# A decoder trunk on one core: recurrent weights split ahead of time in three feed-forward blocks, x copied on ScalarE in the first, and a bound on pending one-column products

## The chip, the cores and the metric

The kernel runs on one core of one Trainium2 chip. The metric is the device time of one execution in microseconds (us). Beside the timed runs there is a profile of one execution. Engine names are those of the profile: PE is TensorE's matmuls, PEld its weight loads, DVE is VectorE, ACT is ScalarE, POOL is GpSimd, SP issues nearly all DMAs.

## The reference, cut to what matters

The input x is 512 tokens by 1024. Two layers, each with a half-weighted SwiGLU, a mixer, and another half-weighted SwiGLU. The mixer of layer 0 is attention, that of layer 1 is RWKV-7 time mixing.

```
def swiglu(h, w_gate, w_up, w_down):
    return (jax.nn.silu(h @ w_gate) * (h @ w_up)) @ w_down      # 1024 -> 2816 -> 1024

for layer in range(2):
    x = x + 0.5 * swiglu(rms_norm(x, ffn_norm[layer, 0]), ...)  # blocks 0 and 2
    h = rms_norm(x, mix_norm[layer])
    x = x + (attention(h) if layer == 0 else rwkv7_time_mix(h, ...))
    x = x + 0.5 * swiglu(rms_norm(x, ffn_norm[layer, 1]), ...)  # blocks 1 and 3
```

In order of time the stages are: feed-forward block 0, attention, blocks 1 and 2, time mixing, block 3. `rwkv7_time_mix` multiplies by the matrices w_k, w_v, w_r, w_o, some small ones (w2, a2, g2), and the low-rank (LoRA) matrices w1, a1, g1. Everything is float32.

## The kernel before, in words

**Split operands.** A float32 matrix t is held as two parts, hi (a cast, on ACT) and lo = t - hi (on DVE). A product is three matmuls, hi by hi, hi by lo, lo by hi (`mm3`). Every weight must so be loaded, cast on ACT (L296) and subtracted on DVE (L297) before TensorE uses it. x stays on chip, transposed, as eight chunks of 128 rows by 512 tokens.

**A feed-forward block** (`ffn`, its order written out in `ffn_steps`). The first 256 columns of gate and up are done in four head steps `("s", kk)`, each with two chunks of x: eight products per chunk pair and bank, the sums of x that the later products need (`sums`, L581 to L587, and their split L331, L332), and the squares of the two chunks (L615) with eight one-column products against ones that add them up over the rows (these run as 16 records). After the fourth the scale of each token (`rstd`) is known, and the gated product u of the head follows (L632). The remaining 2560 columns are five tiles of 512. In each a tile of gate and up is formed by a seven-product scheme, a Winograd form of a 2 by 2 block product: products "1", "2", "6", "7", "5", "3", "4" in two halves each, with weights' sums formed on DVE (L293, the "add" operations) and results combined on DVE (L654). L668 is the copy of product "1" out of PSUM; the third bank pair that it empties is the one in which product "2" goes on. Between the halves stand the transposes of the tile before (`turn`, L691, split by L331 and L332) and its down products (`down`, L712 adds them to x). A full tile has 18 steps that take a weight: 14 halves and four down steps, in the order 1a 1b 2a 2b 6a d0 6b 7a d1 7b 5a 5b d2 3a 3b 4a 4b d3. A block has four head steps, 16 steps in the first tile, 18 in each of the next three, 16 in the last and six at its end.

**Work buffers.** `work()` hands out four SBUF buffers in turn, counted by `turn_of` from the start of the block. The head takes 14: four squares, eight for the sums, one for the gate, one for u. So product "1" of each tile (buffer p) gets number 14, the buffer that held the last t of the sums.

**Parking.** The time mixing needs its weights split, too. That is done ahead, inside feed-forward blocks, and the parts go to DRAM. `next_w` counts a turn at every weight step; `park_some` takes one operation out of `park_ops` at every `park_every`-th turn between 13 and 90. An operation is a pair of weight pieces (70 pieces, 35 pairs): SP issues the loads into one shared raw buffer (L202), ACT casts them (L242), DVE subtracts (L243), SP issues two writes of 512 KB (L246). Two more operations, "lora", do four chunks of the LoRA matrices each (L255 loads, L264 on ACT, L265 on DVE, L269 writes); they need `self.v`, the vectors that `rwkv_setup` makes after block 0. All use the same `park_room`: the sixth of ten buffers, and `pair`, which also takes two transposed activations of the last tile. Before, parking is on in blocks 1 and 2 at every fourth turn: two LoRA operations and 17 pairs in block 1, 18 pairs in block 2.

**x at the start of block 0.** x comes in rows of tokens. `turned(c)` transposes chunk c on TensorE (L353) into a PSUM bank and copies it to `self.x[c]` (L356, on DVE); `prep(c)` then makes the scaled parts from the same bank (L572 on ACT, L573 on DVE). Chunks 0 and 1 come ahead of the first products, each later one two chunks ahead.

**Order.** The instructions' order on each engine is set by a scheduler when the kernel is built, by its own model of the times; it respects the data and the `after` edges (order only, no wait between engines). Each engine then works through its queue in that order.

Of the kernel before, what the change touches and what calls it, by code (L numbers as in the profile page):

```python
# [22 lines left out]
NCH = D // P  # L23
# [26 lines left out]
class Trunk:  # L50
# [160 lines left out]
    def plan_parks(self, every):  # L211

        small = [i for i, tag in enumerate(self.wring) if tag == "r"]
        self.park_ops = [("lora", k) for k in range(0, NCH, 4)] if small else []
        self.park_ops += [small[j : j + 2] for j in range(0, len(small), 2)]
        self.park_every = every

    def park_some(self):
        self.park_turn += 1
        if self.park_ops and 12 < self.park_turn <= 90 and self.park_turn % self.park_every == 0:  # L220
            self.park(self.park_ops.pop(0))

    def park(self, which):

# [98 lines left out]
    def mm3(self, out, lhs, rhs, start, stop):  # L323

        mm = self.mm
        self.after(mm(out, lhs[0], rhs[0], start=start, stop=False), self.gate)
        mm(out, lhs[0], rhs[1], start=False, stop=False)
        self.last_mm = mm(out, lhs[1], rhs[0], start=False, stop=stop)

# [4 lines left out]
    def load_x(self):  # L334
        nc = self.nc
        xsrc = self.a["x"][0].rearrange("(b p) d -> p b d", p=P)
        ts = [self.t("xio", [4, 256], 4) for _ in range(4)]
        t = self.t("vecs", [2, P])

        nc.sync.dma_start(t[:32, 0], self.a["ffn_norm"].rearrange("l f (c p) -> (l f c) p", p=P))  # L340
        nc.scalar.dma_start(ts[0], xsrc[:, :, :256])
        self.prefetch(-1, 1)
        self.prefetch(0)
        for i in range(1, 4):
            self.after(nc.scalar.dma_start(ts[i], xsrc[:, :, i * 256 : (i + 1) * 256]), self.last_cast)
        self.prefetch(-1)
        self.name_vectors(t)
        self.spread_vectors(slice(0, 1))

        def turned(c):  # L350
            ps = self.bank("fd", 2)
            for b in range(4):
                nc.tensor.transpose(  # L353
                    ps[:, b * P : (b + 1) * P], ts[c // 2][:, b, (c % 2) * P : (c % 2 + 1) * P], self.ident
                )
            nc.vector.tensor_copy(self.x[c], ps)  # L356
            return ps

        self.turned = turned
# [182 lines left out]
    def ffn(self, gain, done=lambda c: None):  # L542
# [54 lines left out]
        def first(kk):  # L597
# [6 lines left out]
            for k in (2 * kk, 2 * kk + 1):  # L604
                for b in range(4):
                    block = (0, 3)[b // 2] if k < 4 else (1, 2)[b // 2]
                    rhs = tuple(t[:, (k % 2) * S :][:, :S] for t in w)
                    self.mm3(live["s"][b], x_part(k % 4, block, b % 2), rhs, k == 0, k == NCH - 1)
                if turned and k + 2 < NCH:
                    prep(k + 2)  # L610
                if k >= 4:
                    sums(k - 4)
# [3 lines left out]
            for e in range(2):  # L616
                for b in range(4):
                    col = 4 * (c + e) + b
                    self.mm(
                        live["sum"][:, col : col + 1], sq[:, e, b * P : (b + 1) * P], self.ones[:, 0:1],  # L620
                        start=True, stop=True,
                    )
# [7 lines left out]
            for b, ps in enumerate(live["s"]):  # L630
# [2 lines left out]
                    out=u[:, b], in0=ps[:, FIRST:], scalar=rstd[:, b : b + 1], in1=g[:, b], op0=ALU.mult, op1=ALU.mult  # L633
                )
            us[-1] = [u[:, b] for b in range(4)]

        def product(n, q, h):
            if not h:
# [1225 lines left out]
def trunk_kernel(ctx, tc, stop=5, start=0, **aps):  # L1864
# [2 lines left out]
              lambda: t.plan_ffn(1, 0), lambda: t.plan_rwkv(), lambda: t.plan_ffn(1, 1)]  # L1867
    for s in stages[start : stop + 1]:
        s()
    t.plan_parks(4)  # L1870
    t.load_x()
    gains = {(l, f): t.vec["ffn_norm"][:, (2 * l + f) * NCH :][:, :NCH] for l in range(2) for f in range(2)}
    mixg = [t.vec["mix_norm"][:, l * NCH : (l + 1) * NCH] for l in range(2)]
# [13 lines left out]
            t.turned(c)  # L1887
        t.turned = None
    for i in range(start, stop + 1):
        t.parking = i in (2, 3)  # L1890
        if i in (0, 2, 3, 5):
            t.ffn(gains[i // 3, int(i % 3 > 0)], *[t.store_x] * (i == stop))
        elif i == 1:
# [34 lines left out]
```

## Time and profile before

| | |
|---|---|
| timed runs, us | 2142.15, 2133.08, 2140.88 (median 2140.88) |
| the profiled execution, us | 2135.13 |
| its span, us | 2133.2 |
| mean granted TensorE clock | 0.987 |
| feed-forward matmuls | block 0 from 8.0 to 379.0; blocks 1 and 2 from 626.9 to 1366.2; block 3 from 1755.5 to 2126.0 |
| TensorE busy in 0 to 400 us, 600 to 1010, 1010 to 1380, 1750 to 2133 | 385.2, 389.1, 364.7, 374.3 us |

The table's times of the blocks come from the timeline of TensorE, the last row from windows. An engine that is "busy" is in an instruction; a weight load (PEld) overlaps the matmuls. A wait in brackets after an instruction of the timeline is the idle time of its engine just before it, with what ended it.

### The profile page before, as it was taken

The page shows a single profiled execution, that of the slowest core. Times are in us where ns is not written, and L with a number is a line of the kernel's source. Part 1 is how long each engine was busy: PE and PEld are TensorE (multiplying, and loading weights), DVE is VectorE, ACT ScalarE, POOL GpSimd, SP SyncE. Part 2 cuts the span into 40 slices and gives each one's busy share as a digit, 9 for nine tenths or more (in the row PEclk, how much of TensorE's full clock was granted, in tenths as well). Part 3 has the DMA queues.
Part 4 walks back from the last instruction along what each step waited for, and adds up shares of the span by engine and source line. Part 5 has one row for each costly group of instructions (what it writes and reads, how often), then busy time and mean ns, then how long its engine had stood idle before and what let it go on. Part 6 is the DMA issues. An engine that isn't in the chain of part 4 may idle for free.

```text
span 2133.2 us, 29169 instructions
## 1 busy us (share of the span) xinstructions
PE 2048.1 (96%) x11527; PEld 1639.8 (77%) x11527; DVE 1585.9 (74%) x1981; ACT 954.4 (45%) x1381; POOL 123.4 (6%) x165
## 2 busy tenths in 40 slices
PE   8999999999989999999999999999898999999998
PEld 6788888776877788877878888777566668888887
DVE  6778786467777888887798888556966557887784
ACT  5433443354335554444544444373634425433342
POOL 0000000211000000000000000112322100000000
PEclk9999999999989999999999999999989999999999
DMA  5333332421113468763255674536654332333321
GB/s 169 89 115 103 99 99 72 125 79 51 52 47 100 147 221 275 237 207 128 62 196 197 211 235 158 207 112 191 213 135 104 91 120 83 109 99 119 109 89 40
DMA packets 219296, 282.41 MB, mean 132 GB/s; under 512 B 45395, under 2 KB 135659, under 8 KB 219160
## 3 DMA queue, kind: packets, MB, share of 16 engines
q1 hardware_dynamic: 216520, 278.20, 41.4%
q10 hardware_dynamic: 2640, 2.36, 0.3%
q8 instruction: 91, 1.49, 0.3%
q14 instruction: 45, 0.37, 0.1%
HBM read 227.76 MB, written 54.59 MB: 132 GB/s over the span
## 4 chain that ended last, share of the span: by engine, by line
PE 77%; DVE 11%; DMA 5%; ACT 3%; issue 2%; SPq 1%; POOL 0%; DVEq 0%; ACTq 0%
PE fp L120 36%; PE fd L120 18%; PE am L120 7%; PE rm L120 4%; PE rq L120 2%; DVE parts L297 2%; PE wo L120 2%; DMA const<-in_ffn_w_up_dram 1%; PE rl L120 1%; PE rr L120 1%; DVE const L1601 1%; DVE wx L293 1%; DVE const L1607 1%; ACT parts L296 1%; PE fd L691 1%
## 5 line engine op out<-in xcount | busy, mean ns | idle before, releaser
L120 PE MATMUL fp<-parts,xs 128*128 128x512 f32 x2016 | 493.1, 393 | 13.2 <-DVE parts L297 9.0
L120 PEld LDWEIGHTS fp<-parts,xs 128*128 128x128 f32 x2016 | 377.6, 189 | 96.6 <-DVE parts L297 12.0
L120 PE MATMUL fd<-act,parts 128*128 128x512 f32 x1728 | 409.4, 390 | 2.5 <-DVE acts L332 1.6
L296 ACT CAST parts<-wx 128x1024 fp32r<-128x1024 f32 x224 | 233.6, 1051 | 349.9 <-PE fp L120 174.6
L120 PEld LDWEIGHTS fd<-act,parts 128*128 128x128 f32 x1728 | 323.7, 188 | 72.6 <-DVE acts L332 3.4
L297 DVE TENSOR_TENSOR parts<-wx,parts 128x1024 fp32r<-128x1024 f32 x224 | 271.8, 1220 | 73.2 <-ACT parts L296 73.1
L296 ACT CAST parts<-const 128x1024 fp32r<-128x1024 f32 (+1 forms) x192 | 198.2, 1033 | 262.0 <-PE fp L120 134.0
L120 PE MATMUL fp<-parts,xb 128*128 128x512 f32 x1152 | 291.3, 400 | 9.6 <-ACT wx L668 6.8
L297 DVE TENSOR_TENSOR parts<-const,parts 128x1024 fp32r<-128x1024 f32 (+1 forms) x192 | 229.5, 1197 | 59.4 <-ACT parts L296 54.3
L120 PEld LDWEIGHTS fp<-parts,xb 128*128 128x128 f32 x1152 | 216.8, 191 | 56.1 <-ACT wx L668 7.4
L654 DVE TENSOR_TENSOR wx<-fp,wx 128x1024 f32<-128x1024 f32 x140 | 168.7, 1218 | 30.0 <-PE fp L120 28.8
L712 DVE SCALAR_TENSOR_TENSOR const<-fd,const 128x512 f32<-128x512 f32 x160 | 108.4, 685 | 77.6 <-PE fd L120 77.4
L120 PE MATMUL fp<-parts,xa 128*128 128x512 f32 x576 | 145.0, 400 | 4.3 <-ACT xa L572 2.6
L120 PEld LDWEIGHTS fp<-parts,xa 128*128 128x128 f32 x576 | 110.2, 193 | 29.2 <-ACT xa L572 3.3
L120 PE MATMUL am<-xg,parts 128*128 128x512 f32 x384 | 99.4, 410 | 0.0
L416 POOL TENSOR_TENSOR ssum<-ssum,sq 128x512 f32<-128x512 f32 x14 | 23.0, 1646 | 1198.3 <-ACT sq L415 1197.9
L120 PEld LDWEIGHTS am<-xg,parts 128*128 128x128 f32 x384 | 72.0, 191 | 25.6 <-issue 9.9
L102 ACT ACTIVATE wx<-wx,const 128x512 f32<-128x512 f32 x80 | 53.5, 716 | 43.7 <-DVE wx L654 43.6
L242 ACT CAST acts<-wx 128x1024 fp32r<-128x1024 f32 (+2 forms) x37 | 37.1, 1004 | 68.4 <-DMA wx<-in_rw_wk_dram 18.3
L243 DVE TENSOR_TENSOR acts<-wx,acts 128x1024 fp32r<-128x1024 f32 (+2 forms) x37 | 42.9, 1162 | 24.5 <-ACT acts L242 24.5
L120 PE MATMUL rm<-xm,parts 128*128 128x512 f32 x252 | 60.8, 394 | 0.0
L331 ACT CAST act<-fd 128x512 fp32r<-128x512 f32 x80 | 43.7, 587 | 37.3 <-PE fd L691 37.1
(316 smaller groups left out, 2632.9 us busy)
## 6 DMA issues: line engine op xcount, KB each, us to landing
wx<-in_ffn_w_down_dram SPq DMA_DIRECT2D x72, 512.0 KB
parts<-acts SPq DMA_DIRECT2D x68, 512.0 KB
parts<-parts SPq DMA_DIRECT2D x68, 512.0 KB
wx<-in_ffn_w_gate_dram SPq DMA_DIRECT2D x44, 512.0 KB
wx<-in_ffn_w_up_dram SPq DMA_DIRECT2D x40, 512.0 KB
const<-in_ffn_w_up_dram SPq DMA_DIRECT2D x40, 512.0 KB
const<-in_ffn_w_gate_dram SPq DMA_DIRECT2D x36, 512.0 KB
const<-in_ffn_w_down_dram SPq DMA_DIRECT2D x16, 512.0 KB
```

The costliest lines, as they stand in the source:

```text
L102: ins = nc.scalar.activation(out, in_, func, **kw)
L120: return self.pe(self.nc.tensor.matmul(*args, **kw))
L242: nc.scalar.copy(hi, src)
L243: nc.vector.tensor_tensor(out=lo, in0=src, in1=hi.bitcast(F32), op=ALU.subtract)
L293: self.nc.vector.tensor_tensor(out=out, in0=in0, in1=in1, op=ALU.add)
L296: self.last_cast = self.nc.scalar.copy(hi[:r, :n], raw[:, :n])
L297: self.nc.vector.tensor_tensor(out=lo[:r, :n], in0=raw[:, :n], in1=hi[:r, :n].bitcast(F32), op=ALU.subtract)
L331: self.nc.scalar.copy(hi, t)
L416: nc.gpsimd.tensor_tensor(out=ssum, in0=ssum, in1=sq, op=ALU.add)
L654: add = lambda out, other, ps=ps: nc.vector.tensor_tensor(out=out, in0=ps, in1=other, op=ALU.add)
L691: nc.tensor.transpose(ps[:, b * P : (b + 1) * P], us[n][b][:, f * P : (f + 1) * P], self.ident)
L712: nc.vector.scalar_tensor_tensor(out=self.x[c], in0=ps, scalar=0.5, in1=self.x[c], op0=ALU.mult, op1=ALU.add)
```

## The change: parking in three blocks, copies on ScalarE, an order edge and a skipped buffer

- `plan_parks` keeps the LoRA operations in a list of their own, and the step is 6 turns instead of 4. Parking is on in blocks 0, 1 and 2. `park_some` takes a LoRA operation first, once `self.v` is there, that is from block 1 on. With turns 18, 24, ... 90 this makes 13 pairs in block 0, two LoRA operations and 11 pairs in block 1, and 11 pairs in block 2.
- `turned` copies x out of PSUM on ScalarE instead of VectorE.
- An order edge on TensorE: the first product of head step kk comes after the last one-column product of head step kk - 2, so that no more than sixteen one-column products are pending.
- After the head, one work buffer is skipped: the tiles' p, q, v and r each take the buffer after the one they had. p then has the buffer of the last squares.

```diff
     def plan_parks(self, every):
         small = [i for i, tag in enumerate(self.wring) if tag == "r"]
-        self.park_ops = [("lora", k) for k in range(0, NCH, 4)] if small else []
-        self.park_ops += [small[j : j + 2] for j in range(0, len(small), 2)]
+        self.park_ops = [small[j : j + 2] for j in range(0, len(small), 2)]
+
+        self.lora_ops = [("lora", k) for k in range(0, NCH, 4)] if small else []
         self.park_every = every

     def park_some(self):
         self.park_turn += 1
-        if self.park_ops and 12 < self.park_turn <= 90 and self.park_turn % self.park_every == 0:
-            self.park(self.park_ops.pop(0))
+        ops = self.lora_ops if self.lora_ops and hasattr(self, "v") else self.park_ops
+        if ops and 12 < self.park_turn <= 90 and self.park_turn % self.park_every == 0:
+            self.park(ops.pop(0))
...
-        self.after(mm(out, lhs[0], rhs[0], start=start, stop=False), self.gate)
+        self.first_mm = self.after(mm(out, lhs[0], rhs[0], start=start, stop=False), self.gate)
...
-            nc.vector.tensor_copy(self.x[c], ps)
+            nc.scalar.copy(self.x[c], ps)
...
                     self.mm3(live["s"][b], x_part(k % 4, block, b % 2), rhs, k == 0, k == NCH - 1)
+                    if k == 2 * kk and not b:
+                        self.after(self.first_mm, live.get(("sq", kk - 2)))
...
-                    self.mm(
+                    live["sq", kk] = self.mm(
                         live["sum"][:, col : col + 1], sq[:, e, b * P : (b + 1) * P], self.ones[:, 0:1],
...
             us[-1] = [u[:, b] for b in range(4)]
+
+            next(turn_of)
...
-    t.plan_parks(4)
+    t.plan_parks(6)
...
-        t.parking = i in (2, 3)
+        t.parking = i in (0, 2, 3)
```

## The prediction

> **What bounds the kernel now.** I read the page first (busy shares and the chain), then windows over equal work in the four feed-forward blocks, then the timeline of single engines where a block is longer than the others.
>
> ```profile
> span 2133.2 us, 29169 instructions
> PE 2048.1 (96%) x11527; PEld 1639.8 (77%) x11527; DVE 1585.9 (74%) x1981; ACT 954.4 (45%) x1381; POOL 123.4 (6%) x165
> PE 77%; DVE 11%; DMA 5%; ACT 3%; issue 2%; SPq 1%; POOL 0%; DVEq 0%; ACTq 0%
> ```
>
> TensorE is busy 96% of the span. A change that removes no matmul can win only the stretches in which TensorE idles or runs below its clock. The change touches only the feed-forward blocks (blocks 0 to 3 in order of time). A window from the same product to the last product of each shows how much there is. The columns are the stretch, its length, then busy time and count for PE, PEld, DVE, ACT and POOL, then the granted clock, the DMA share and GB/s.
>
> ```profile
> 72.55:378.95 306.40, 304.08 (x1379) 251.07 (x1377) 238.93 (x253) 125.42 (x144) 6.61 (x4) 1.00 0.33 99
> 686.30:1007.60 321.30, 309.87 (x1378) 252.04 (x1377) 267.50 (x322) 155.66 (x218) 0.00 (x0) 0.99 0.61 198
> 1054.60:1366.20 311.60, 306.77 (x1378) 250.99 (x1377) 254.33 (x262) 138.97 (x160) 6.85 (x5) 1.00 0.60 197
> 1816.90:2126.10 309.20, 306.48 (x1396) 253.01 (x1396) 230.52 (x239) 115.97 (x131) 0.00 (x0) 1.00 0.30 91
> ```
>
> PE does 1378 or 1379 products in the first three (the fourth has some of the output's transposes too), so the lengths compare. Blocks 0 and 3 park nothing; against block 0, block 1 is 14.9 us longer and block 2 is 5.2 us longer. Parking therefore costs 20.1 us in all today. The heads of the blocks (72 products each) differ as well:
>
> ```profile
> 45.90:72.50 26.60, 22.26 (x101) 17.59 (x101) 19.49 (x31) 16.10 (x22) 0.00 (x0) 0.94 0.14 40
> 661.20:686.30 25.10, 21.28 (x97) 17.68 (x96) 18.08 (x26) 15.95 (x21) 0.00 (x0) 0.86 0.21 64
> 1034.80:1054.60 19.80, 19.36 (x98) 16.01 (x97) 14.60 (x21) 11.33 (x16) 0.00 (x0) 1.00 0.16 46
> 1796.40:1816.90 20.50, 19.40 (x97) 16.01 (x96) 14.95 (x22) 12.41 (x17) 0.00 (x0) 1.00 0.20 57
> ```
>
> Against block 3's 20.5 us, block 0's head loses 6.1 us and block 1's 4.6 us. These two and the 20.1 us are all that the change can reach: 30.8 us, 1.4% of the span.
>
> **The copies of x in block 0 move from DVE to ACT.** Eight instructions. The price on DVE is the row of L356; the price on ACT is that of the only like copy, L751's 128x512 PSUM copy.
>
> ```profile
> L356 DVE COPY const<-fd 128x512 f32<-128x512 f32 x8 | 5.5, 687 | 6.7 <-PE fd L353 6.7
> L751 ACT COPY xout<-fd x7: 585/586/593, 2118.1 to 2127.6; 128x512 f32<-128x512 f32 x7
> 47.31 0.63 PE L353 MATMUL fd<-const,xio 128*128 128x128 f32 x4 [0.23 <-DVE xb L573]
> 50.02 0.68 DVE L356 COPY const<-fd 128x512 f32<-128x512 f32 x1
> 50.74 0.69 ACT L572 ACTIVATE xb<-fd,const 128x512 fp32r<-128x512 f32 x1 [0.21 <-DVE const L356]
> 51.48 1.20 PE L120 MATMUL fp<-parts,xb 128*128 128x512 f32 x4 [1.71 <-ACT xb L572]
> 53.23 2.11 PE L120 MATMUL fp<-parts,xb 128*128 128x512 f32 x8 [0.55 <-DVE xb L573]
> 57.81 1.01 ACT L668 COPY wx<-fp 128x1024 f32<-128x1024 f32 x1 [0.34 <-DVE xs L332]
> 58.87 7.33 PE L120 MATMUL fp<-parts,xb 128*128 128x512 f32 x24 [1.85 <-ACT wx L668]
> ```
>
> DVE loses 5.5 us and ACT gains 8 x 0.586 = 4.7 us. In the head ACT is busy 16.10 of 26.60 us, so it has the room. What matters is the chain: the transposes end at 47.94 and the copy starts only at 50.02, because DVE works through its queue; L572 starts exactly when the copy ends, and TensorE waits 1.71 us for it. On ACT the copy and L572 follow each other and that queue is out of the chain. I take from this the waits of 1.71, 0.55 and 0.23 = 2.5 us. The last wait of the head, 1.85 us, ends with L668, which waited for DVE's last split of the sums; with DVE lighter by the copies of this stretch I take 1.4 us of it, and 0.6 us of the slow 24 products behind it (7.33 us, against 5.75 in a row below). That is 4.5 us. The bounds are 6.1 us (the head becomes block 3's) and a loss of 1.2 us: two copies of 0.586 us now stand ahead of the first casts on ACT. I take none of that loss, since the operands there come late by DMA; the cover is this wait, and without it the first products start later:
>
> ```profile
> 14.49 1.05 ACT L296 CAST parts<-const 128x1024 fp32r<-128x1024 f32 x1 [4.20 <-DMA const<-in_ffn_w_up_dram]
> ```
>
> Queued behind a copy on ACT are the weights' casts; a copy waits for its transposes, and DVE's second half of each split waits for ACT.
>
> **One work buffer is skipped after the head.** The copy of the first product (L668) then goes to the buffer of the last squares, free after their 16 one-column matmuls, and no longer to that of the last sums, free after DVE's L332. In block 1:
>
> ```profile
> 666.65 1.84 PE L120 MATMUL fd<-const,wx 128*128 128x1 f32 x16
> 669.28 1.22 DVE L332 TENSOR_TENSOR xs<-wx,xs 128x1024 fp32r<-128x1024 f32 x1
> 669.95 1.28 ACT L98 ACT_TABLE_LOAD   x1
> 671.25 1.01 ACT L668 COPY wx<-fp 128x1024 f32<-128x1024 f32 x1
> 672.31 7.80 PE L120 MATMUL fp<-parts,xb 128*128 128x512 f32 x24 [3.82 <-ACT wx L668]
> 675.65 1.90 DVE L632 SCALAR_TENSOR_TENSOR wx<-fp,const,wx 128x256 f32<-128x256 f32 x4 [0.34 <-ACT wx L102]
> 1804.96 5.75 PE L120 MATMUL fp<-parts,xb 128*128 128x512 f32 x24 [1.10 <-ACT wx L668]
> ```
>
> The squares are read by 668.5, DVE ends at 670.50, and a table load then stands ahead of the copy. Freed earlier, the copy can start near 669, about 2.2 us sooner, and the 3.82 us shrink to 1.6. Late next is the gated product u (L632, ends at 677.55), for which TensorE's next transposes wait, so I take no more than 2.2 us. Bounds: 0 (the order on ACT stays) and 4.6 us. In block 3 L668 already waits for TensorE, and I take nothing there. The clock is the open part: 24 products took 7.80 us behind the 3.82 us wait and 5.75 us behind a wait of 1.10.
>
> The Trainium skill ("TensorE: Matmul & The Clock Gate", HAM oscillation) says that TensorE drops to its slow clock in gaps of more than about 3.4 us. By it a wait cut to 1.6 us would give back the 2.05 us of clock as well, and block 1's term would be 4.3 us, an estimate; but block 0's 1.85 us wait ought to have cost no clock, and the trace disagrees there (7.33 us). I stay with 2.2 us.
>
> **One-column products, at most sixteen pending.** The first product of the third and fourth pair now comes behind the sums two pairs earlier. In block 1 both sums came a moment late:
>
> ```profile
> 643.27 1.75 PE L120 MATMUL fp<-parts,xb 128*128 128x512 f32 x7
> 644.86 3.63 PE L120 MATMUL fd<-const,wx 128*128 128x1 f32 x32
> ```
>
> Sixteen of these 32 records move ahead of seven products, 1.6 us. The order is on TensorE itself, the work is the same, and the squares that they read were written earlier. Zero; the bounds are 1.6 us either way.
>
> **Parking.** 35 pairs and two LoRA steps of four chunks each. Before, every fourth turn: 2 LoRA and 17 pairs in block 1, 18 in block 2. After, every sixth turn from 18 to 90: 13 pairs in block 0, 2 LoRA and 11 pairs in block 1, 11 in block 2. The number of operations and DMAs stays. Their rows:
>
> ```profile
> L242 ACT CAST acts<-wx 128x1024 fp32r<-128x1024 f32 (+2 forms) x37 | 37.1, 1004 | 68.4 <-DMA wx<-in_rw_wk_dram 18.3 <-DMA wx<-in_rw_wv_dram 16.5 <-DMA wx<-in_rw_wr_dram 11.0
> L243 DVE TENSOR_TENSOR acts<-wx,acts 128x1024 fp32r<-128x1024 f32 (+2 forms) x37 | 42.9, 1162 | 24.5 <-ACT acts L242 24.5
> ACT acts L264 <- DMA lora<-acts: 12.2, 6, 5.2
> 737.81 4.38 PE L120 MATMUL fp<-parts,xs 128*128 128x512 f32 x11 [1.83 <-DVE parts L297]
> 745.05 2.81 PE L120 MATMUL fp<-parts,xs 128*128 128x512 f32 x11 [1.76 <-DVE parts L297]
> 225.00:250.00 25.00, 25.00 (x120) 20.80 (x119) 22.64 (x24) 11.46 (x14) 0.00 (x0) 1.00 0.20 57
> 1207.00:1232.00 25.00, 24.43 (x115) 19.84 (x113) 24.76 (x27) 13.55 (x16) 0.00 (x0) 1.00 0.52 168
> 768.00:865.00 97.00, 96.34 (x436) 79.23 (x435) 86.55 (x88) 46.79 (x51) 0.00 (x0) 1.00 0.69 233
> 768.00:865.00 97.00, 10.53 (x10) 1.00 0.69 233
> 1082.00:1107.00 25.00, 22.70 (x101) 17.82 (x100) 24.30 (x25) 11.23 (x13) 0.00 (x0) 1.00 0.39 124
> ```
>
> A pair costs ACT 1.0 us and DVE 1.16 us, and ACT stood 68.4 us before these casts with the weights' casts queued behind. The LoRA chunks share one room, so each waits for the write before it. I give the LoRA 6.5 us of block 1's 14.9: waits of 1.83 and 1.76, 1.57 of slow clock (4.38 less 2.81), some 1.3 around. It stays: eight serial chunks still cover the next tile's crowded part. The other 13.6 us (8.4 and 5.2) are 35 pairs at 0.39 us.
>
> The crowded part is the stretch from the first to the sixth of the block products: DVE is busy 24.76 of 25 us with parking, 22.64 without. So block 0 has 2.36 us of slack there, two splits' worth. At a flat 0.39 us the move costs 13 x 0.39 = 5.1 us in block 0 and returns 5.1 us in blocks 1 and 2; for that slack I take 1 us of gain. Bounds: 5.1 us of gain (block 0 hides them all), and 4.1 us of loss, if each of block 0's four tiles lost what block 2's worst tile did (25.00 less 22.70 = 2.3 us; 9.2 less 5.1). SP's queue carries 13 pairs' loads and writes more in block 0, where DMA is busy 0.33 against 0.61 and 0.60 in the windows above. The parking at turn 90 shares a buffer with the last tile's transposed activations; its write must land first. It has no row before, and I cost it 0, with up to 2 us in each of two blocks inside the bounds.
>
> **Sum.** 4.5 + 2.2 + 0 + 1.0 = 7.7 us. The profiled execution took 2135.1 us, the median of the runs is 2140.9, the other runs 2133.1 and 2142.2: the four have a mean of 2137.8, the profiled one 2.7 below. 2137.8 less 7.7 gives 2130 us (2127 for an execution like the profiled one, 2133 for one like the median).
>
> **Rivals.** *Parking spreads better than flat.* The waits come from bunches: at a third fewer in a block each finds its room free. If block 0 hides its 13 and blocks 1 and 2 drop by half of their 13.6 us: 6.8 + 6.7 = 13.5, 2124 us. Against it: the second row for 768 to 865 counts L242 alone: ten casts in 97 us, and TensorE lost only 0.66 us.
>
> *The heads don't move.* The scheduler orders ACT anew; a copy caught behind a cast that waits for its weights costs what DVE's queue cost. The heads give 0 to 1 us: 2137 us. For it: ACT's casts in the head also wait for DMA and TensorE; against it: 10.5 us of ACT idle there.
>
> *Slower: parking at one fixed place.* A tile has 18 steps and 6 divides 18, so in every full tile a parking falls on the second half of the second product, just ahead of the crowded part, where every fourth step wandered. Eleven such tiles (4, 3, 4) at block 2's 2.3 us are 25.3 us against 13.6 now: 11.7 more, less 6.7 of the heads, 2143 us. It decides from 1.85 us a tile. Against it: the tiles of the 97 us stretch.
>
> **How the numbers follow.** Forecast 0.45, better spread 0.22, heads unmoved 0.20, fixed place 0.13. A measurement tells about 0.5% here, 10.7 us: faster means under 2130.2. The forecast lies on that edge and gives 0.24 faster and 0.21 same; the spread is faster; the unmoved heads are same; the fixed place gives 0.07 same and 0.06 slower. Together 0.46, 0.48, 0.06. Range 2118 (both heads whole at 10.7, 5.1 of parking, and 4 of the runs' own scatter) to 2143 (the fixed place).
>
> **What would show it.** Copies: block 0's head window near 22 us and no wait on L572. Buffer: L668 in block 1 before 669.5. Parking: the window of block 0 from 306.4 to about 310, block 1's from 321.3 to about 318, block 2's to about 309; DVE waits at the first half of the sixth product in every tile would speak for the fixed place. I am wrong if the other stages move by more than 3 us, or if block 0 grows by more than 9.

## The result and the profile after

The changed kernel takes 2149.9 us (median of 8 runs, 2145.8 to 2156.6); the kernel before takes 2142.0 (8 runs, 2133.1 to 2145.5). The ratio is 1.0044, interval 1.0032 to 1.0055: slower by 8 us between the medians (9 us by the ratio), where 7.7 us of gain were forecast, and outside the range of 2118 to 2143. The two profiled executions differ by more, 2135.1 against 2150.1, because that of before lay 6.9 us under its own median and that of after at its median; in which stages those 6.9 us lie, no run tells. Medians and ratios leave out two executions of the experiments that took 6152.6 us (no90_q) and 11232 us (crowd).

The page of the changed kernel, the lines that answer to the first fence of the prediction:

```profile
span 2147.9 us, 29168 instructions
PE 2057.7 (96%) x11527; PEld 1645.2 (77%) x11527; DVE 1581.6 (74%) x1973; ACT 957.0 (45%) x1389; POOL 123.5 (6%) x165
PE 74%; DVE 14%; ACT 5%; DMA 4%; issue 2%; SPq 1%; POOL 0%; DVEq 0%; ACTq 0%; POOLq 0%
```

In the chain DVE has 14% for 11% and ACT 5% for 3%, although DVE's own work shrank (1585.9 to 1581.6 us). TensorE waits more often for the two engines that split weights. The windows of the changed kernel over the same products as in the prediction: the heads of blocks 0 and 1, then the bodies of blocks 0 to 2.

```profile
44.10:66.90 22.80, 21.64 (x103) 17.75 (x103) 18.17 (x27) 15.81 (x22) 0.00 (x0) 0.93 0.16 47
669.70:695.90 26.20, 22.91 (x97) 18.36 (x96) 17.18 (x25) 15.62 (x21) 0.00 (x0) 0.87 0.20 61
66.90:387.50 320.60, 309.96 (x1379) 252.11 (x1377) 251.80 (x266) 136.95 (x157) 6.56 (x4) 0.99 0.50 158
695.90:1019.20 323.30, 311.68 (x1378) 253.93 (x1377) 261.42 (x318) 149.99 (x212) 0.00 (x0) 0.98 0.52 168
1066.10:1379.70 313.60, 306.89 (x1378) 251.03 (x1377) 247.21 (x255) 132.25 (x153) 6.85 (x5) 1.00 0.51 161
```

Block 0's head won 3.8 us (26.60 to 22.80), and began 1.8 us earlier. Its body lost 14.2 us (306.40 to 320.60). Blocks 1 and 2, with a third fewer parked pairs, did not get shorter: each lost 2.0 us. Block 1's head lost 1.1 us. Time mixing, which the change does not touch, took 2.1 us more, and block 3's body took 1.1 us less (308.10 us, from 1832.50 to 2140.60). These come to 14.7 us, the whole difference of the spans.

**Block 0's end** is 5.6 us of the 14.2. From the 1321st to the 1393rd product of the block it takes 25.1 us, before 19.6. The timeline of the changed kernel there; in brackets, the idle time just before the instruction and what ended it:

```profile
341.07 1.12 SPq L202 DMA_DIRECT2D wx<-in_rw_wv_dram  x2
348.28 1.05 ACT L244 CAST acts<-wx 128x1024 fp32r<-128x1024 f32 x1 [5.25 <-DMA wx<-in_rw_wv_dram]
349.36 1.23 DVE L245 TENSOR_TENSOR acts<-wx,acts 128x1024 fp32r<-128x1024 f32 x1 [3.11 <-ACT acts L244]
351.64 1.22 DVE L660 TENSOR_TENSOR wx<-fp,wx 128x1024 f32<-128x1024 f32 x1
353.91 0.74 DVE L669 SCALAR_TENSOR_TENSOR wx<-wx,const 128x512 f32<-128x512 f32 x1
354.71 1.95 PE L697 MATMUL fd<-const,wx 128*128 128x128 f32 x6 [3.25 <-DVE wx L669]
```

The row that TensorE names is L669, but the cause stands three steps back. The pair parked at turn 90 is loaded only at 341.07, and its cast is already at the head of ACT's queue when ACT falls idle at 343.03. ACT stands 5.25 us for the transfer, the subtraction behind it holds DVE for 3.11 us, and L660 and L669, which the last tile needs, come after that. TensorE waits 3.25 us, and its next products run at a low clock (0.79 from 357.1 to 366.0 us).

**The tiles** are the other 8.6 us (14.2 less 5.6). One of them, the changed kernel's DVE and TensorE:

```profile
111.71 1.22 DVE L245 TENSOR_TENSOR acts<-wx,acts 128x1024 fp32r<-128x1024 f32 x1
119.72 1.22 DVE L299 TENSOR_TENSOR parts<-wx,parts 128x1024 fp32r<-128x1024 f32 x1
120.99 2.80 PE L120 MATMUL fp<-parts,xs 128*128 128x512 f32 x11 [1.45 <-DVE parts L299]
```

DVE works without a gap from 109.25 to 123.3. The parked pair's L245 is one of these operations, and eight operations later TensorE waits 1.45 us for a split. Over block 0's body the waits of TensorE for this split at the block products grew from 1.3 us, one wait (L297 before), to five:

```profile
PE fp L120 <- DVE parts L299: 4.4, 5, 1.4
```

They stand where product "6" begins, in every tile from the second on: 0.83 and 1.45 us there (115.25 and 120.99 us), then 0.70, 0.70 and 0.69 (183.18, 246.35, 309.37 us). The rest of the 8.6 us are smaller waits and longer records of the products, which were not taken apart.

**Block 1's head.** The copy out of PSUM (L674 after) did come earlier, and the gain was spent on the next thing:

```profile
675.15 1.84 PE L120 MATMUL fd<-const,wx 128*128 128x1 f32 x16
677.08 1.01 ACT L674 COPY wx<-fp 128x1024 f32<-128x1024 f32 x1 [0.69 <-PE fd L120]
677.92 7.36 PE L120 MATMUL fp<-parts,xb 128*128 128x512 f32 x24 [0.93 <-DVE const L630]
685.83 0.44 PE L697 MATMUL fd<-const,wx 128*128 128x128 f32 x2 [0.55 <-DVE wx L636]
688.07 0.70 PE L697 MATMUL fd<-const,wx 128*128 128x128 f32 x4 [1.81 <-DVE wx L636]
```

The copy starts 0.1 us after the sums of the squares (before: 2.8 us after, 668.49 to 671.25), and the wait of 3.82 us is 0.93. But between two tiny steps of the scale (L447 at 681.35, L448 at 683.70) DVE now does two weight sums, so the gated product u is late and the transposes wait 0.55 and 1.81 us. The head as a whole got 1.1 us longer.

### The profile page after: what moved, and what is told of

Read it like the earlier page. It is cut to its first block, busy times and chain, and to the rows that moved or that the text cites. A ratio compares the mean times of both kernels' runs of the same rounds, so it can differ in the third digit from the quotient of the medians.

```text
span 2147.9 us, 29168 instructions
## 1 busy us (share of the span) xinstructions
PE 2057.7 (96%) x11527; PEld 1645.2 (77%) x11527; DVE 1581.6 (74%) x1973; ACT 957.0 (45%) x1389; POOL 123.5 (6%) x165
## 4 chain that ended last, share of the span: by engine, by line
PE 74%; DVE 14%; ACT 5%; DMA 4%; issue 2%; SPq 1%; POOL 0%; DVEq 0%; ACTq 0%; POOLq 0%
PE fp L120 36%; PE fd L120 18%; PE am L120 7%; DVE parts L299 3%; PE wo L120 2%; PE rq L120 2%; PE rr L120 1%; PE rm L120 1%; DMA const<-in_ffn_w_up_dram 1%; DVE wx L295 1%; DVE const L1607 1%; DVE const L295 1%; ACT parts L298 1%; DVE const L1613 1%; PE fd L697 1%
## 5 line engine op out<-in xcount | busy, mean ns | idle before, releaser
L120 PE MATMUL fp<-parts,xs 128*128 128x512 f32 x2016 | 499.0, 395 | 19.2 <-DVE parts L299 12.4
L120 PEld LDWEIGHTS fp<-parts,xb 128*128 128x128 f32 x1152 | 216.5, 191 | 51.8 <-ACT wx L674 2.8
L660 DVE TENSOR_TENSOR wx<-fp,wx 128x1024 f32<-128x1024 f32 x140 | 169.0, 1219 | 24.8 <-PE fp L120 24.5
L102 ACT ACTIVATE wx<-wx,const 128x512 f32<-128x512 f32 x80 | 53.5, 717 | 64.0 <-DVE wx L660 63.9
L244 ACT CAST acts<-wx 128x1024 fp32r<-128x1024 f32 (+2 forms) x37 | 37.0, 1004 | 88.8 <-DMA wx<-in_rw_wk_dram 26.2
L245 DVE TENSOR_TENSOR acts<-wx,acts 128x1024 fp32r<-128x1024 f32 (+2 forms) x37 | 43.0, 1164 | 33.7 <-ACT acts L244 33.7
L697 PE MATMUL fd<-const,wx 128*128 128x128 f32 x352 | 56.5, 276 | 8.9 <-DVE wx L669 4.9
```

The source lines that it names most:

```text
L102: ins = nc.scalar.activation(out, in_, func, **kw)
L120: return self.pe(self.nc.tensor.matmul(*args, **kw))
L244: nc.scalar.copy(hi, src)
L245: nc.vector.tensor_tensor(out=lo, in0=src, in1=hi.bitcast(F32), op=ALU.subtract)
L660: add = lambda out, other, ps=ps: nc.vector.tensor_tensor(out=out, in0=ps, in1=other, op=ALU.add)
L697: nc.tensor.transpose(ps[:, b * P : (b + 1) * P], us[n][b][:, f * P : (f + 1) * P], self.ident)
```

## The experiments

The table shows one execution of each, in us. A block's 1464 weight products are counted in order: "head" runs from the start of the 97th to that of the 169th, "body" from there to that of the last, "mixing" from block 2's last to block 3's 97th. These marks begin and end at starts, so a body is 0.3 to 0.4 us less than in the windows.

| | head 0 | body 0 | head 1 | body 1 | body 2 | mixing | span |
|---|---|---|---|---|---|---|---|
| before | 26.6 | 306.1 | 25.1 | 320.9 | 311.2 | 430.6 | 2133.2 |
| after | 22.7 | 320.3 | 26.2 | 322.9 | 313.2 | 432.7 | 2147.9 |
| heads | 22.8 | 306.0 | 22.5 | 318.6 | 311.7 | 438.3 | 2128.3 |
| parks | 26.4 | 319.4 | 22.7 | 319.5 | 312.9 | 433.1 | 2145.5 |
| clear | 22.7 | 307.8 | 26.4 | 314.5 | 311.4 | 442.8 | 2134.4 |
| crowd | 22.7 | 316.2 | 22.8 | 320.1 | 317.8 | 437.9 | 2147.1 |
| no90 | 22.7 | 315.4 | 26.1 | 324.8 | 317.1 | 447.7 | 2161.8 |
| early | 22.8 | 313.6 | 23.3 | 315.3 | 310.5 | 432.9 | 2129.5 |
| heads_q | 22.7 | 306.1 | 22.6 | 319.5 | 311.5 | 434.1 | 2125.7 |
| clear_q | 22.7 | 307.8 | 26.4 | 314.8 | 311.7 | 435.8 | 2126.6 |
| copies | 26.5 | 309.4 | 24.5 | 319.0 | 313.3 | 433.2 | 2137.5 |
| skip | 25.9 | 306.2 | 26.4 | 318.4 | 311.7 | 435.3 | 2137.9 |
| all | 22.8 | 311.1 | 25.1 | 317.7 | 317.9 | 432.7 | 2134.4 |

Block 0's body by pieces, in us: tiles 1 to 4 (tile 0 is the first) from the starts of the 313th, 577th, 841st and 1105th product, the end from the 1321st to the 1393rd.

| | tile 1 | tile 2 | tile 3 | tile 4 | end |
|---|---|---|---|---|---|
| before | 63.3 | 61.7 | 61.7 | 50.8 | 19.6 |
| after | 66.0 | 63.6 | 63.2 | 53.3 | 25.1 |
| clear | 63.3 | 62.4 | 62.4 | 50.9 | 19.6 |
| crowd | 69.5 | 62.4 | 63.4 | 52.3 | 19.6 |
| early | 65.3 | 65.4 | 62.6 | 51.8 | 19.6 |
| no90 | 64.7 | 63.2 | 62.5 | 53.5 | 22.6 |

The theory after the result was that parking in block 0, at places fixed by the step of six, costs more than the heads bring; the rivals were that the pair at turn 90 with its shared buffer is all of the loss, and that late loads are, wherever the pairs stand.

### heads: the change without its parking

```diff
-        ops = self.lora_ops if self.lora_ops and hasattr(self, "v") else self.park_ops
+        ops = self.park_ops
-    t.plan_parks(6)
+    t.plan_parks(4)
-        t.parking = i in (0, 2, 3)
+        t.parking = i in (2, 3)
```

(The LoRA operations are first in `park_ops` again.)

> The changed kernel with the parking of before (blocks 1 and 2, every fourth turn, LoRA first); the copies on ScalarE, the order edge and the skipped buffer stay. Theory 1 (the parking brought the whole loss, the heads won): block 0's head (72 products) 22.7 us against 26.6, its start 1.8 us earlier, everything behind as before: 5 to 7 us under before, ratio about 0.997. Theory 2 (a part of the loss comes from the head edits, by a new order elsewhere): no faster than before, block 1's head 26.2 us as in the changed kernel.

Measured: 2133.3 us, ratio to before 0.9953 (0.9938 to 0.9968). Its window of block 0's body:

```profile
67.20:373.60 306.40, 304.29 (x1379) 251.09 (x1377) 239.06 (x253) 125.53 (x144) 6.60 (x4) 1.00 0.33 99
```

To the hundredth the length of before. The head edits win about 10 us by the ratio and cost block 0's body nothing.

### parks: the parking alone

```diff
-            nc.scalar.copy(self.x[c], ps)
+            nc.vector.tensor_copy(self.x[c], ps)
-                    if k == 2 * kk and not b:
-                        self.after(self.first_mm, live.get(("sq", kk - 2)))
-            next(turn_of)
```

> The changed kernel with the copies of x back on VectorE, no order edge and no skipped buffer: the new parking alone. Theory 1: block 0's head as before (26.6 us), block 0's body 320 us against 306, in all about 15 us over before, ratio about 1.007. Theory 2 (the two halves of the change hurt each other): ratio under 1.003.

Measured: 2153.3 us, 1.0050 (1.0036 to 1.0064), between the two theories' 1.007 and 1.003. Its window of block 0's body:

```profile
71.20:391.00 319.80, 310.63 (x1379) 253.63 (x1377) 252.13 (x266) 137.56 (x157) 6.62 (x4) 0.98 0.50 158
```

Block 0's body grows by 13.4 us without any head edit, and the bodies of blocks 1 and 2 change by -1.4 and +1.7 us. So block 0's loss is the parking's. Block 1's head is 22.7 us here, without the skipped buffer, and 26.4 us in skip, with it: what that head takes is decided by the order that the scheduler finds, not by the skip.

The two halves do not add up. By the ratios heads is 10 us under before and parks 11 us over, yet both together are 9 us over. Block 1 shows a part of it: head and body together take 346.0 us before, 341.1 in heads, 342.2 in parks, and 349.1 with both. No run tells why; the cause of block 1's 3.1 us stays open.

### clear and crowd: as many pairs, at other turns

```diff
-        if ops and 12 < self.park_turn <= 90 and self.park_turn % self.park_every == 0:
+        if ops and self.park_turn in (13, 17, 27, 30, 33, 45, 48, 51, 63, 66, 69, 81, 84):     # clear
+        if ops and self.park_turn in (14, 22, 24, 25, 40, 42, 43, 58, 60, 61, 76, 78, 79):     # crowd
```

> The changed kernel, its 13 parkings in each block moved to the turns 13, 17, 27, 30, 33, 45, 48, 51, 63, 66, 69, 81, 84: in each full tile the steps 6b, 7b and d2, behind the crowded stretch of VectorE, and none at the last two halves. Theory 1 (a fixed place ahead of the sixth product's sums is what costs): block 0's body from 320 back to 308 to 311 us, blocks 1 and 2 each 3 to 6 us shorter than in the changed kernel, in all 15 to 22 us under it, which is under before. Theory 2 (each pair has its price wherever it runs, 0.4 to 1 us): block 0's body stays within 3 us of 320, less the 5.6 us at its end.

> The changed kernel, its parkings moved to the turns 14, 22, 24, 25, 40, 42, 43, 58, 60, 61, 76, 78, 79: in tiles 1 to 4 the steps 1b, 2b and 6a, all three in the crowded stretch. Theory 1 (the place costs): each of the four tiles loses 3 to 5 us at its sixth product instead of 1.2 to 1.9, block 0's body 322 to 328 us though nothing is parked at its end. Theory 2 (each pair has its price wherever it runs): block 0's body about 314 us, the changed kernel's 320 less the 5.6 us of its end.

Measured: clear 2137.9 us, 0.9982 (0.9965 to 1.0000); crowd 2145.5 us, 1.0020 (1.0003 to 1.0038). The window of clear over block 0's body, and its group of parked casts in that window:

```profile
67.40:375.60 308.20, 304.99 (x1379) 250.80 (x1377) 251.83 (x266) 136.58 (x157) 6.69 (x4) 1.00 0.50 164
```

```profile
L244 ACT CAST acts<-wx 128x1024 fp32r<-128x1024 f32 x13 | 13.7, 1053 | 42.2 <-DMA wx<-in_rw_wk_dram 17.0 <-DMA wx<-in_rw_wv_dram 12.4 <-issue 6.0
```

The same group in the changed kernel, over the same products:

```profile
L244 ACT CAST acts<-wx 128x1024 fp32r<-128x1024 f32 x13 | 13.6, 1048 | 35.8 <-DMA wx<-in_rw_wk_dram 26.2 <-DMA wx<-in_rw_wv_dram 8.0 <-DMA wx<-in_rw_a_dram 1.5
```

Both park 13 pairs in block 0 with the same DVE work (251.83 and 251.80 us), and clear's body is 12.4 us shorter: 5.5 us at the end, where clear parks nothing, and 7 us in the tiles. ACT even stands idle longer ahead of the parked casts in clear (42.2 against 35.8 us), so neither the number of pairs nor the idle time in front of a cast is the price. The place is. The total came down by 12 us and not by the expected 15 to 22, because time mixing took 10 us more. Block 2's body is 1.8 us under the changed kernel's, where 3 to 6 were expected.

Crowd does not show that the crowded stretch is the bad place. For block 0's body 322 to 328 us were expected of the place and about 314 of a price per pair; it took 316.2, 10.1 over before, and its end 19.6. Of the 10.1 us 6.1 are in tile 1. Tiles 2 to 4 lose 0.7, 1.7 and 1.5 us with three pairs each in the stretch; the changed kernel, with one of three there, loses 1.9, 1.5 and 2.5. So the places differ in price, but which of the changed kernel's places is the dear one stays open.

### early and no90: the load or the last turn alone

```diff
+        if ops is self.park_ops and ops and 12 < self.park_turn <= 90 and self.park_turn % self.park_every == 3:
+            self.park_load(ops[0])                  # early: loads three turns ahead, the rest as in the change
-        if ops and 12 < self.park_turn <= 90 and self.park_turn % self.park_every == 0:
+        if ops and 11 < self.park_turn <= 84 and self.park_turn % self.park_every == 0:      # no90
```

> The changed kernel with each pair's loads issued three turns ahead (turns 15, 21, ... 87); casts, subtractions and writes stay at the turns 18, 24, ... 90. The LoRA steps are as they were. Theory 1 (the cast stands at the head of ACT's queue until its load has landed, and the weights' casts stand behind it): ACT's idle time before the parking casts falls from 88.8 us to under 45, block 0's body from 320 to 310 to 314 us, its end from 25.1 to under 21.5. Theory 2 (the price is the work itself, 1.0 us on ACT and 1.2 us on DVE in a crowded stretch): block 0's body stays within 3 us of 320.

> The changed kernel with parking at the turns 12, 18, ... 84 instead of 18, 24, ... 90: the one parking at the last step (4b of the last tile) goes to the middle of the first tile, all others stay. Theory 1 (at turn 90 a cast waits for its load at the head of ACT's queue, ahead of the last tile's gated product): the 72 products before the last 71 take 19.6 us instead of 25.1 in block 0 and instead of 22.6 in block 1, 8 to 9 us in all less the price of a parking elsewhere, so 4 to 8 us under the changed kernel. Theory 2 (the end of block 0 is long because attention's weights and the DMAs of its tables now share the queue with 13 parkings): block 0's end stays above 23 us.

Measured: early 2131.3 us, 0.9942 (0.9921 to 0.9963); no90 2159.9 us, 1.0065 (1.0039 to 1.0090). The window of early over block 0's body, and TensorE at the end of it:

```profile
68.00:382.00 314.00, 307.89 (x1379) 251.93 (x1377) 252.03 (x266) 137.07 (x157) 6.67 (x4) 0.99 0.49 161
```

```profile
354.03 3.03 PE L120 MATMUL fd<-act,parts 128*128 128x512 f32 x12 [0.40 <-DVE acts L343]
```

The wait of 3.25 us is gone and the end takes 19.6 us again, with the pair of turn 90 still parked and the buffer still shared. But the edit moved more than the loads. The scheduler put the casts earlier, too; that of turn 90 in early:

```profile
333.40 1.05 ACT L253 CAST acts<-wx 128x1024 fp32r<-128x1024 f32 x1 [2.81 <-DMA wx<-in_rw_wv_dram]
```

It stands behind the 1267th product, in the changed kernel behind the 1332nd, and ACT's 2.81 us in front of it cost TensorE nothing there. So the late load held ACT in the changed kernel (the 5.25 us in its trace), but load and place of the cast were not varied apart, nor was the buffer. ACT's idle time ahead of all parked casts fell from 88.8 to 59.9 us, not to under 45 as expected. The tiles keep their price: 313.6 less 306.1 leaves 7.5 of the 8.6 us. Block 1 takes 10.5 us less over head and body (338.6 against 349.1), of which the head's 2.9 may be the scheduler's, and the ratio to before goes from 1.0044 to 0.9942.

no90 came out slowest of all. Block 0's body is 4.9 us shorter than the changed kernel's, but its end is not the expected 19.6 us:

```profile
343.40:366.00 22.60, 20.70 (x89) 16.08 (x89) 11.80 (x15) 8.39 (x10) 0.00 (x0) 0.92 0.17 51
```

The last parked cast of this block runs at 317.09. At the end TensorE goes to the last tile's transposes after 12 down products, as in the changed kernel, and waits 0.17, 0.60 and 0.72 us among and behind them (from 348.89); the 12 products behind take 4.59 us at a clock of 0.63. In early, and in the kernel before, 20 and 24 down products come first, then all eight transposes in one run (from 351.05 and 348.07), and those 12 products take 3.03 and 3.01 us. Block 1's end takes 22.6 us as in the changed kernel. So the end is 3.0 us over before without any parked pair in it, and taking turn 90 away returned 2.5 us of the 5.6 in block 0 and nothing in block 1. Beside this, block 2 is 3.9 us longer than in the changed kernel, and time mixing 15.0 us, which the edit does not touch. That led to the next runs.

### heads_q, clear_q and no90_q: the order of one queue held

In time mixing SP issues, for the last chunk, two loads of `vcd` that TensorE needs. SP in clear:

```profile
1629.18 2.39 SPq L1638 DMA_DIRECT2D us<-uout  x4
1631.62 1.55 SPq L1673 DMA_DIRECT2D const<-vcd  x2
```

TensorE in clear:

```profile
1634.30 0.45 PE L120 MATMUL rr<-const 64*64 64x64 f32 x2 [7.93 <-DMA const<-vcd]
```

SP in the kernel before:

```profile
1630.99 1.25 SPq L1667 DMA_DIRECT2D const<-vcd  x2
1633.38 0.93 SPq L1622 DMA_DIRECT2D const<-tout  x2
1638.05 2.17 SPq L1632 DMA_DIRECT2D us<-uout  x4
```

Before, the `vcd` loads come ahead of the return loads of `tout` and `uout`. In clear they come behind, and those wait for a write and a copy; TensorE waits 7.93 us (8.03 in no90 at the same place, 2.69 in heads). The scheduler had re-ordered a stage that no edit touched. The three runs hold the order of before:

```diff
-        weave(recur, ((6, 7), bonus[1]), ((2, 5, 8, 11, 14, 20, 21, 22, 23), inverse))
+        weave(recur, ((6, 7), bonus[1]), ((2, 5, 8, 11, 14, 19, 20, 21, 22, 23), inverse))
...
-        nc.sync.dma_start(du, U)
+        if sg:
+            yield
+        self.after(nc.sync.dma_start(du, U), self.vcd_load if sg else None)
```

(The loads of `t0` get the same edge; `vcd_load` is the last load of `vcd`.)

> The run heads (new head edits, parking as before) with SP's order in the time mixing held as in the kernel before: the loads of the last chunk's centred v (const<-vcd) ahead of the reload of the inverse's result, by an order edge and one more step of the generator. Theory 1 (the time mixing is longer there, 438 us against 431 from block 2's last product to block 3's 97th, because the scheduler put those loads behind DMAs that wait): 431 us again, 5 to 7 us under heads, ratio 0.992 to 0.994. Theory 2 (the stretch varies from run to run): 435 to 440 us, as heads.

> The run clear (all of the change, the parking behind the crowded stretch) with the same order held in the time mixing. Theory 1: the stretch from block 2's last product to block 3's 97th goes from 443 to 431 us, 10 to 12 us under clear, ratio to before 0.992 to 0.994. Theory 2 (run to run): about 440 us, ratio 0.997 to 1.0.

> The run no90 (parking at the turns 12 to 84) with SP's order in the time mixing held as in the kernel before. Theory 1 (no90 lost in the time mixing, where the loads of the last centred v stood behind DMAs that wait, 8.0 us on TensorE and the inverse behind it): the stretch from block 2's last product to block 3's 97th goes from 448 to 433 to 437 us, 10 to 14 us under no90, ratio to before 1.000 to 1.002. Theory 2 (run to run): as no90.

Measured: heads_q 2129.4 us, 0.9935 (0.9919 to 0.9952); clear_q 2127.3 us, 0.9925 (0.9903 to 0.9947); no90_q 2149.5 us, 1.0040 (1.0026 to 1.0055). Time mixing fell from 438.3 to 434.1 and from 442.8 to 435.8 us (431 was expected of both), the blocks stayed within 1 us. clear_q is the fastest of all. Its advantage over heads_q is within the intervals. The ratio of clear fell from 0.9982 to 0.9925, that of no90 from 1.0065 to 1.0040 (there the intervals overlap; 1.000 to 1.002 was expected). This is the changed kernel's 1.0044, so leaving out turn 90 alone repairs nothing that a run can tell. No trace of no90_q is used here.

### copies and skip: one head edit at a time

```diff
-            nc.vector.tensor_copy(self.x[c], ps)
+            nc.scalar.copy(self.x[c], ps)            # copies: before, with this alone
...
+            next(turn_of)                            # skip: before, with this alone
```

> The kernel before with one edit: the copies of x in block 0 on ScalarE. Theory 1 (the chain transposes, DVE's copy, L572 held TensorE in block 0's head): head 22.7 us against 26.6, its start 1 to 2 us earlier, everything behind as before: 4 to 6 us under before, ratio 0.997 to 0.998. Theory 2 (the head wins only together with the skipped buffer, which frees L668): head 24 to 25 us, ratio 0.999.

> The kernel before with one edit: a work buffer skipped after the head. Theory 1 (L668 waits in block 1 for the last split of the sums): block 1's head 22.5 to 23 us against 25.1. Theory 2 (what is late next is u, through the small VectorE operations of the scale that the scheduler puts between the weights' sums): block 1's head 25 to 26.5 us, the wait moved from L668 to the transposes of u. Block 0's head 25 to 26.6 either way.

Measured: copies 2139.2 us, 0.9987 (0.9977 to 0.9998); skip 2137.6 us, 0.9978 (0.9968 to 0.9987). Neither shortens block 0's head much (26.5 and 25.9 us; of the copies 22.7, or 24 to 25, were expected), and together, in heads, they make it 22.8. In copies, DVE, ACT and TensorE:

```profile
54.90 1.23 DVE L332 TENSOR_TENSOR xs<-wx,xs 128x1024 fp32r<-128x1024 f32 x1
56.28 1.01 ACT L668 COPY wx<-fp 128x1024 f32<-128x1024 f32 x1
57.35 6.50 PE L120 MATMUL fp<-parts,xb 128*128 128x512 f32 x21 [5.21 <-ACT wx L668]
```

In the changed kernel, ACT and TensorE at the same places:

```profile
45.78 0.59 ACT L358 COPY const<-fd 128x512 f32<-128x512 f32 x1 [0.73 <-PE fd L355]
46.26 0.70 ACT L574 ACTIVATE xb<-fd,const 128x512 fp32r<-128x512 f32 x1
45.50 4.81 PE L120 MATMUL fp<-parts,xb 128*128 128x512 f32 x20
53.23 7.12 PE L120 MATMUL fp<-parts,xb 128*128 128x512 f32 x23 [1.16 <-ACT wx L674]
```

The copies do what they were forecast to do: copy and L572 follow each other, the 20 products run through, the waits of 1.71 and 0.55 us are gone. But TensorE then arrives earlier at the wait for L668, which without the skip must wait for L332 (ends 56.13) and stands behind a table load on ACT (54.99 to 56.27): 5.21 us instead of 1.85. The skipped buffer takes that away (1.16). The copies alone move the wait; with the skip it goes. In block 1 the skip alone gives 26.4 us, with a wait of 2.22 us for u in place of most of the 3.82. The order edge was in heads but not run alone, so its share stays open. In copies, body 0 is 3.3 us longer as well, at one tile; I did not follow that.

### all: clear's turns, loads two turns ahead, the order held

```diff
+        if ops is self.park_ops and ops and self.park_turn + 2 in (13, 17, 27, ..., 84):
+            self.park_load(ops[0])                   # on top of clear_q
```

> All of the change, the parking at the turns of the run clear, each pair's loads issued two turns ahead, and SP's order in the time mixing held. Theory 1 (place and late load are two separate prices): blocks 0, 1 and 2 at 306 to 307, 312 to 314 and 309 to 310 us, 2 to 5 us under clear_q, ratio 0.990 to 0.992. Theory 2 (behind the crowded stretch a late load costs nothing, since little stands behind the cast): as clear_q, 0.992 to 0.994.

Measured: 2136.4 us, 0.9979 (0.9969 to 0.9989): slower than clear_q, where 0.990 to 0.994 were expected. Blocks 0, 1 and 2 lost 3.3, 2.9 and 6.2 us. SP, ACT and TensorE in block 2 of this run:

```profile
1099.09 2.72 SPq L202 DMA_DIRECT2D wx<-in_ffn_w_down_dram  x2
1106.05 1.04 ACT L307 CAST parts<-wx 128x1024 fp32r<-128x1024 f32 x1 [7.48 <-DMA wx<-in_ffn_w_down_dram]
1107.95 1.06 ACT L342 CAST act<-fd 128x512 fp32r<-128x512 f32 x2
1110.14 8.10 PE L120 MATMUL fd<-act,parts 128*128 128x512 f32 x24 [4.82 <-DVE act L343]
```

SP and ACT at the same place in clear_q:

```profile
1093.15 3.83 SPq L202 DMA_DIRECT2D wx<-in_ffn_w_down_dram  x2
1096.96 1.06 ACT L333 CAST act<-fd 128x512 fp32r<-128x512 f32 x2
1099.97 2.00 ACT L298 CAST parts<-wx 128x1024 fp32r<-128x1024 f32 x2 [1.95 <-DMA wx<-in_ffn_w_down_dram]
```

The loads of the down weights are no later in the run all: they go out beside the block's 374th product, in clear_q beside the 373rd, and their cast follows 7.0 and 6.8 us after. The order on ACT differs. In the run all, the cast that waits for them stands ahead of the casts of the transposed activations (L342), in clear_q behind them (L333); so ACT's 7.48 us hold up the activations, too, and TensorE waits 4.82 us for these. That is 4.82 of block 2's 6.2 us. The other losses were not followed, and no run tells whether the earlier loads or merely a new order brought them.

## Why the prediction was wrong, step by step

**Copies on ACT (-4.5 in block 0's head).** The size came out, by luck: 3.8 us in the head and 1.8 us of an earlier start, inside the bounds. The reason was half right. The 2.5 us of L572's and L573's waits went. The 1.4 us of the last wait and its clock were credited to a lighter DVE; alone, the copies make that wait 3.4 us longer, and the head stays at 26.5 us. It was the skipped buffer that paid there, for which the prediction took nothing in block 0.

**Skipped buffer (-2.2 in block 1's head).** The mechanism was right: the copy followed the sums by 0.1 us. But the head got 1.1 us longer, outside the bounds of 0 and 4.6 us of gain. The step that failed is "late next is u": it was named, and then charged no wait beyond 1.6 us, although the order of DVE's small steps is the scheduler's to change.

**Order edge (0).** Not isolated.

**Parking (-1.0).** Here the prediction broke, twice. The step that failed first is the flat 0.39 us a pair. It was a mean over places: it made 13 pairs in block 0 cost 5.1 us, less 1 for the slack, and made blocks 1 and 2 give 5.1 us back. Measured: block 0 gave up 14.2 us, 8.6 of them in the tiles, and blocks 1 and 2 returned nothing but took 2.0 each. In block 0 the price goes by the place (clear against after, 7 us in the tiles with equal work). In blocks 1 and 2 the 13.6 us that were divided by 35 pairs were the excess over block 0, and no run leaves these blocks without parking. Block 2's body in clear, with 11 pairs, is as long as before with 18 (311.60 us in the prediction's window):

```profile
1044.40:1356.20 311.80, 306.46 (x1378) 250.99 (x1377) 246.96 (x255) 130.78 (x153) 6.84 (x5) 1.00 0.49 162
```

So that these 5.2 us are the pairs' at all was never shown. Second, turn 90 was costed 0, with up to 2 us for the shared buffer. Block 0's end took 5.6 us more. In the trace it is the late load at the head of ACT's queue, for which the prediction had the row (68.4 us of ACT idle ahead of L242) and did not ask what was queued behind it at the end of a block. Taking turn 90 away returned 2.5 us of the 5.6, though the late load was gone; TensorE's order there, transposes before the last down products, kept the rest. Block 1's end (22.6 us, before 21.2) did not get shorter by it.

**The rivals.** The fixed place came nearest: 2.3 us a tile forecast, 2.15 found in block 0 (8.6 over four tiles), over its decision point of 1.85. It gave 2143 us; the 5.6 us at block 0's end and the 3.3 us by which block 1's head missed its forecast were not in it. It got 0.13 because of one stretch of 97 us in which TensorE lost 0.66 us, but there the pairs stood at every fourth turn and wandered. A stretch at other places is no evidence against a fixed one. "Better spread" is refuted by after and nearly reached in block 0 by clear (1.8 us over before), with places chosen by hand. "The heads don't move" is refuted by heads.

**The signs.** "Block 0's head near 22 and no wait on L572": right. "Block 0 to 310, block 1 to 318, block 2 to 309": 320.6, 323.3, 313.6. "DVE waits at the first half of the sixth product in every tile would speak for the fixed place": they are there, 0.69 to 1.45 us each. "Wrong if block 0 grows by more than 9": it grew by 14.2. "Wrong if the other stages move by more than 3": time mixing moved 2.1 us here, but between the experiments 430.6 to 447.7, which is more than any term of the sum; no step of the prediction looked at what a new schedule does to a stage that no edit touches.

The Trainium skill ("TensorE: Matmul & The Clock Gate", HAM oscillation) ties the low clock to gaps of more than about 3.4 us; the prediction stayed with the trace against it. That was right: behind a wait cut to 0.93 us the 24 products of block 1's head still took 7.36 us (7.80 before).

## What to carry to other kernels

Equal background work cost 1.8 us at one set of places and 14.2 at another: before moving such work, list for each new place what stands behind it on each engine's queue, and when its data lands. A cast that waits for its load holds up whatever is queued behind it (5.25 us at block 0's end, 7.48 us in the run all), be it background work or not. Edits that each shorten a block alone can lengthen it together (block 1: 341.1 and 342.2 us alone, 349.1 together, 346.0 before). When a scheduler orders the whole kernel, compare the untouched stages first, and hold their order before judging an edit of under 1%.

## What the runs showed of the hardware

The granted clock fell behind some stretches in which TensorE did no product of 512 columns, though it was busy for 1.4 to 1.8 us of them. Windows of the changed kernel: the one-column products with the wait behind them, the 23 products after that, and a part of these alone:

```profile
50.30:53.20 2.90, 1.77 (x17) 1.69 (x16) 2.90 (x5) 2.06 (x2) 0.00 (x0) 1.00 0.02 6
53.20:60.30 7.10, 7.07 (x24) 5.67 (x25) 5.64 (x13) 5.33 (x9) 0.00 (x0) 0.76 0.00 0
53.67:57.08 3.41, 3.41 (x10) 2.63 (x9) 2.97 (x8) 3.04 (x6) 0.00 (x0) 0.50 0.00 0
```

And of no90 at block 0's end: a stretch with only transposes, and the 12 products behind it:

```profile
349.00:351.80 2.80, 1.37 (x9) 0.66 (x7) 2.09 (x4) 2.79 (x4) 0.00 (x0) 1.00 0.13 39
353.20:357.80 4.60, 4.57 (x13) 3.62 (x14) 0.57 (x1) 0.00 (x0) 0.00 (x0) 0.63 0.00 0
```

But of the kernel before at block 1's end, with the same transposes and nearly the same waits:

```profile
975.40:978.48 3.08, 1.36 (x10) 0.65 (x8) 2.37 (x4) 3.05 (x5) 0.00 (x0) 1.00 0.09 29
979.80:982.90 3.10, 3.05 (x13) 2.55 (x14) 0.59 (x1) 0.00 (x0) 0.00 (x0) 1.00 0.00 0
```

So the length of such a stretch does not decide alone: 2.8 and 2.9 us were followed by a clock of 0.63 and 0.76, 3.08 us by full speed, and the longest wait in any of them was 1.16 us. The fall itself has one form at three places of the changed kernel: the clock is 0.50 for 3.41 us or twice that (53.67 to 57.08, 354.04 to 360.87, 678.31 to 681.72), and full on both sides. The three starts lie whole steps of 3.413 us apart (88 and 95 steps). That the fall is decided once in such a step, and a stretch hits or misses it by where it lies, would account for both outcomes; no run moved a stretch to try it. A step at half clock costs up to 1.7 us of products (an estimate, half of 3.41), near the 1.6 us between 7.33 or 7.36 and 5.75 us for 24 products. The 7.33 us behind the 1.85 us wait, which the prediction had to leave open, would be such a step: with the 16 one-column products in front of it the stretch without a full product was 3.5 us long (55.34 to 58.87).
